# Ordering loaded operands of small products behind dense steps in a fused attention, RWKV and delta-rule block

## The chip, the core and the metric

The kernel runs on one core of one Trainium2 chip. The metric is the device time of one execution in microseconds, as the median of three runs. TensorE (PE in the rows) does the matrix products, VectorE (DVE), ScalarE (ACT) and GpSimd (POOL) the elementwise work, and SyncE (SP) issues most of the DMAs.

## What is computed

One block of a hybrid model: 1024 tokens, width 1024. The input is normed and projected by one large matrix (8176 columns); its columns feed three mixers (sparse attention "NSA" with 8 heads, an RWKV-7 recurrence with 8 heads, and a gated delta rule "GDN" with 4 heads) and three gates. The gated sum of the mixers is projected, added to the input, and a feed-forward layer of width 4096 follows. All in float32.

```python
proj = rms(x) @ w_in                       # nsa | rwkv | gdn | gates
# NSA: three branches per query; one over compressed keys and values
blk = t[:, :, cmp_idx, :] + cmp_pos[j]     # 63 windows of 32 tokens
hid = silu(blk.reshape(B, G, n_cmp, 32 * Dh) @ cmp_w1[j])
kc, vc = rms(hid @ cmp_w2[0]), hid @ cmp_w2[1]
ks, kw = rms(k_s), rms(k_w)                # selected and window branch
# GDN, per chunk
decay = exp(where(lower, gam[:, None] - gam[None, :], -inf))
a_mat = eye(C) + where(strict, (kb @ k.T) * decay, 0)
u, w = solve(a_mat, v * beta), solve(a_mat, kb * exp(gam))
qk = (q @ k.T) * decay
# RWKV: a state per head, a rank-one correction per token
# then
merged = g0 * (o_a @ wb0) + g1 * (o_b @ wb1) + g2 * (o_c @ wb2)
x = x + merged @ w_out
x = x + relu(rms(x) @ w_ff1)**2 @ w_ff2
```

## The kernel before

**Two kinds of work share TensorE.** *Dense steps* are the projections with 512-column products, each split in three products of high and low parts (`fps` tiles, line 97). *Small products* belong to the mixers (`mps` tiles, lines 97 and 101): chains of small matrix products with DVE, ACT or POOL work between them. The mixers are written as Python generators ("tasks"), which `yield` a delay at each point where something else should run. `Block.run` takes the task that is due; where none is due it emits a dense step (three products) instead. The clock of this game, `te.time`, counts estimated TensorE time of what was emitted. So a delay of 3.0 after a load means that about 3 us of dense products are emitted before the next small product. The delays stand in the tables `LAT` (RWKV), `GLAT` (GDN) and `NLAT` (NSA).

**What is emitted is not yet the order.** When the kernel is built, a scheduler sets the order on each engine, by priorities and by its own estimate of durations. Dense steps carry a lower priority (`delta`), so a small product may pass dense steps that were emitted ahead of it. `Tensor.note` adds an edge the other way: the first dense product of a step comes behind the last small one emitted (`anchor`). On the chip each engine works strictly in its order, so a product that waits holds all behind it.

**The stages.** RWKV (about 60 to 645 us of the trace): eight units; in each, a triangular inverse is made of 16-blocks by DVE (`inv_blocks`), written to DRAM and read back as `U16` and `T16`; `mm8(L16, T16)` (rows `T,L`), then `mm8(U16, X)` (rows `L,U`) and more steps widen it to 64-blocks, and four recurrence steps (`VS,AG`, `xs,U`, `VS,KB`, `VS,G`) use it. GDN (to about 1068 us): the same pattern with `gT`, `gX`, `gU` and 128-blocks, `mm4(X, T)` being the first product behind the load (rows `gT,gX`); the recurrence is `gZ,KQ`, `gxh,gU`, `gyb,gKg`. There a POOL step makes `gDs`, the decays without their diagonal, from `gD`. NSA preparation (about 1069 to 1160 us): four `_nsa_kv` tasks load keys and values (`kr`, `vr`, 256 KB each) and norm them (first product `ksq`, then `krb`, `vr`); `_nsa_compress` loads `posr` (16 KB), transposes it, and for keys and values in turn loads `kT` (1 MB), `cw1` (four loads of 512 KB) and `cw2` (64 KB), with 16 products `cw,xl`. Then 32 attention units follow. Dense work of the projection ends during them; the output stage and the feed-forward layer come last.

**Queues.** All loads named here go out on SP, `posr` and `kg` on POOL's queue, stores of finished dense tiles (`gates<-fst`) on ACT's.

## Time and profile before

| | us |
|---|---|
| median of three runs | 2536.28 |
| lowest, highest | 2533.8, 2540.54 |
| the profiled execution | 2527.64 |
| its span, first to last instruction | 2525.9 |
| PE busy in it | 2377.5 |
| mean granted TensorE clock | 0.965 |

The profiled execution took 1.7 us more than its span. A granted clock of 1.00 is 2.4 GHz, 0.5 is 1.2 GHz; a mean between them is a mixture over a stretch. Rows of waits name the engine that waited, what it wanted to do, and what it waited for. "x8" counts records: a float32 product of a small tile leaves two records.

### The profile page before, as it was taken

How to read it: one execution, taken by the hardware profiler on the slowest of the kernel's cores; microseconds unless marked ns; L12 is line 12 of the kernel's file. 1: busy time of each engine (PE TensorE's matmuls, PEld its weight loads, DVE VectorE, ACT ScalarE, POOL GpSimd, SP SyncE). 2: the span in 40 equal slices, each digit the busy share in tenths (PEclk: the TensorE clock that was granted, in tenths of full speed). 3: DMA queues.
4: the chain of work that ended last, by engine and by line, in shares of the span. 5: the costliest groups of instructions: out<-in, count | busy, mean ns of one | idle time of the engine just before them, and what ended most of it. 6: DMA issues, size and time to landing. Idle time of an engine off the chain costs nothing.

```text
span 2525.9 us, 37184 instructions
## 1 busy us (share of the span) xinstructions
PE 2377.5 (94%) x13589; PEld 1907.6 (76%) x13589; DVE 1472.0 (58%) x3197; ACT 1043.1 (41%) x2083; POOL 986.8 (39%) x975
## 2 busy tenths in 40 slices
PE   6979899999988999989999999999999998999999
PEld 4757676777776777777887777778888876788887
DVE  4586877663477567232556777766454436545444
ACT  5333433332344433225657665654332334423232
POOL 4444444333322121224545675344333346233232
PEclk9889889999999999989999999999999999999999
DMA  4222222222223122272213331014232354223232
GB/s 137 68 56 65 58 63 58 71 54 74 72 66 83 43 57 73 83 173 80 64 52 114 111 106 57 21 62 128 92 109 84 117 164 157 75 88 111 83 111 92
DMA packets 319718, 216.79 MB, mean 86 GB/s; under 512 B 78486, under 2 KB 273184, under 8 KB 319536
## 3 DMA queue, kind: packets, MB, share of 16 engines
q1 hardware_dynamic: 308672, 195.63, 27.3%
q10 hardware_dynamic: 9792, 17.83, 2.0%
q8 instruction: 107, 1.75, 0.3%
q0 software_dynamic: 1072, 0.96, 0.2%
q14 instruction: 75, 0.61, 0.1%
HBM read 178.16 MB, written 36.22 MB: 85 GB/s over the span
## 4 chain that ended last, share of the span: by engine, by line
PE 72%; DVE 13%; DMA 6%; ACT 4%; issue 2%; POOL 2%; SPq 0%; ACTq 0%; POOLq 0%; DVEq 0%
PE fps L97 53%; PE mps L97 15%; PE mps L101 3%; DVE inv_p L336 2%; DVE inv_u L338 1%; DVE gacc L882 1%; DVE BK L550 1%; DMA cw<-in_nsa_cmp_w_dram 1%; POOL wlo L259 1%; DMA lb<-inv 1%; ACT P L1349 1%; ACT whi L254 1%; DMA wraw<-in_w_branch_dram 1%; DVE ast L1344 1%; DMA gin<-gates 1%
## 5 line engine op out<-in xcount | busy, mean ns | idle before, releaser
L259 POOL TENSOR_TENSOR wlo<-wraw,whi 128x512 fp32r<-128x512 f32 (+2 forms) x408 | 530.0, 1302 | 878.9 <-ACT whi L254 848.5
L254 ACT CAST whi<-wraw 128x512 fp32r<-128x512 f32 (+1 forms) x408 | 286.6, 705 | 632.1 <-PE fps L97 444.8
L97 PE MATMUL fps<-hTh,whi 128*128 128x512 f32 x1024 | 447.3, 439 | 6.5 <-ACT rraw L424 3.5
L97 PE MATMUL fps<-hTh,wlo 128*128 128x512 f32 x1024 | 415.8, 410 | 1.3 <-POOL wlo L259 1.3
L97 PE MATMUL fps<-hTl,whi 128*128 128x512 f32 x1024 | 416.5, 408 | 0.0
L259 DVE TENSOR_TENSOR wlo<-wraw,whi 128x256 fp32r<-128x256 f32 (+1 forms) x207 | 129.7, 629 | 232.5 <-ACT whi L254 227.0
L97 PEld LDWEIGHTS fps<-hTh,whi 128*128 128x128 f32 x1024 | 200.9, 197 | 48.5 <-ACT rraw L424 3.6
L97 PEld LDWEIGHTS fps<-hTh,wlo 128*128 128x128 f32 x1024 | 200.0, 196 | 47.7 <-POOL wlo L259 2.2
L97 PEld LDWEIGHTS fps<-hTl,whi 128*128 128x128 f32 x1024 | 201.8, 197 | 32.3
L97 PE MATMUL fps<-h2h,whi 128*128 128x512 f32 x512 | 200.0, 391 | 1.3 <-DVE h2l L291 1.3
L1363 POOL TENSOR_SCALAR P<-P,ast 128x64 f32<-128x64 f32 (+5 forms) x128 | 137.2, 1088 | 160.0 <-DVE ast L1356 97.1
L97 PE MATMUL fps<-h2l,whi 128*128 128x512 f32 x512 | 199.6, 390 | 0.0
L97 PE MATMUL fps<-h2h,wlo 128*128 128x512 f32 x512 | 199.4, 390 | 0.0
L97 PE MATMUL fps<-whi,fl 128*128 128x512 f32 x512 | 191.0, 389 | 0.0
L97 PE MATMUL fps<-whi,fh 128*128 128x512 f32 x512 | 189.9, 391 | 0.0
L97 PE MATMUL fps<-wlo,fh 128*128 128x512 f32 x512 | 189.0, 389 | 0.0
L1442 DVE TENSOR_TENSOR acc<-fps,acc 128x512 f32<-128x512 f32 x160 | 106.7, 686 | 101.4 <-PE fps L97 101.0
L1349 ACT ACTIVATE P<-mps,ast 128x128 f32<-128x128 f32 (+4 forms) x256 | 124.9, 494 | 75.3 <-DVE ast L1347 45.5
L1344 DVE TENSOR_REDUCE ast<-mps 128x1 f32<-128x128 f32 (+4 forms) x256 | 109.0, 441 | 56.3 <-PE mps L97 53.5
L1392 DVE TENSOR_TENSOR PL<-mps,PH 128x512 fp32r<-128x512 f32 (+2 forms) x168 | 103.3, 619 | 47.7 <-ACT PH L1391 47.0
L1391 ACT CAST PH<-mps 128x512 fp32r<-128x512 f32 (+2 forms) x168 | 88.1, 533 | 63.5 <-PE mps L101 58.1
L97 PEld LDWEIGHTS fps<-h2h,whi 128*128 128x128 f32 x512 | 96.2, 188 | 21.5 <-DVE h2l L291 1.8
(465 smaller groups left out, 4802.0 us busy)
## 6 DMA issues: line engine op xcount, KB each, us to landing
wraw<-in_w_in_dram SPq DMA_DIRECT2D x152, 256.0 KB, 2.9
wraw<-in_w_ff_dram SPq DMA_DIRECT2D x128, 256.0 KB, 2.8
wraw<-in_w_ff_dram SPq DMA_DIRECT2D x64, 512.0 KB, 3.4
gates<-fst ACTq DMA_DIRECT2D x48, 256.0 KB, 2.0
wraw<-in_w_branch_dram SPq DMA_DIRECT2D x48, 256.0 KB, 3.2
gin<-gates SPq DMA_DIRECT2D x48, 256.0 KB, 3.2
wraw<-in_w_out_dram SPq DMA_DIRECT2D x16, 512.0 KB, 3.5
nsa_in<-fst ACTq DMA_DIRECT2D x20, 256.0 KB, 2.1
```

What stands on the lines that cost most here:

```text
L97: return self.note(self.nc.tensor.matmul(out, lhsT=lhsT, rhs=rhs, **kw))
L101: return self.note(self.nc.tensor.transpose(out, x, ident))
L254: nc.scalar.copy(hi, raw)
L259: eng.tensor_tensor(out=lo[:, x], in0=raw[:, x], in1=hi[:, x].bitcast(F32), op=OP.subtract)
L336: nc.vector.tensor_tensor(out=v, in0=lt[:n, s, None, s + 1:].to_broadcast([n, w, w]), in1=u[:n, s + 1:, s + 1:].rearrange("p t c -> p c t" ...
L338: nc.vector.tensor_reduce(out=u[:n, s, s + 1:], in_=v, axis=AX, op=OP.add)
L1344: nc.vector.tensor_reduce(out=(mx if i == 0 else mx2)[:, b:b + 1], in_=ps[:, :n], axis=AX, op=OP.max, negate=True)
L1349: nc.scalar.activation(out=Pt[:, c:c + n], in_=tiles[i][:, :n], func=AF.Exp, bias=mx[:, b:b + 1], accum_out=(sm if i == 0 else sm2)[:, b:b ...
L1363: eng.tensor_scalar(out=Pt[:, c:c + n], in0=Pt[:, c:c + n], scalar1=r[:, b:b + 1], scalar2=None, op0=OP.mult)
L1391: nc.scalar.copy(PH[:n, x0:x1], ps[:n, x0:x1])
L1392: tt(out=PL[:n, x0:x1], in0=ps[:n, x0:x1], in1=PH[:n, x0:x1].bitcast(F32), op=OP.subtract)
L1442: tt(out=acc[:, st, c0:c0 + 512], in0=ps, in1=acc[:, st, c0:c0 + 512], op=OP.add)
```

## The change

It has five parts.

1. `Tensor` gets a flag `held` and remembers the last dense product (`filled`). A task sets `held` when the operand of its next small product was loaded by DMA; that product is then placed behind the last dense product emitted before it. It is set at five points: RWKV's `mm8(L16, T16)`, GDN's `mm4(X, T)`, the norm of `kr`, the first `cw,xl`, and the norm of a query `q`.
2. `NLAT[1]` (behind the loads of `kr`, `vr`) goes from 3 to 8, `NLAT[2]` (behind the loads of the compression) from 6 to 14.
3. The compression's task moves from fifth place (order 4) to second (order 0.5), ahead of three of the four `_nsa_kv` tasks.
4. `posr` is loaded with the constants at the kernel's start.
5. GDN's `gDs` goes; `gD`, which keeps its diagonal, takes its place. `triS` goes with it.

```diff
-NLAT = (1.5, 3.0, 6.0, 0.3, 1.0, 3.0, 6.0, 0.6, 2.0, 0.8)
+NLAT = (1.5, 8.0, 14.0, 0.3, 1.0, 3.0, 6.0, 0.6, 2.0, 0.8)
@@ class Tensor
-        self.last = self.anchor = None
-        self.dense = False
+        self.last = self.anchor = self.filled = None
+        self.dense = self.held = False
@@ def note(self, ins)
         if not self.dense:
             self.fresh = ins.ins
-        elif self.anchor is not None:
+            if self.held and self.filled is not None:
+                self.tc.add_manual_dep(ins.ins, self.filled.name, self.EDGE, reason="behind the dense steps emitted before it")
+            self.held = False
+            return ins
+        self.filled = ins.ins
+        if self.anchor is not None:
             self.tc.add_manual_dep(ins.ins, self.anchor.name, self.EDGE, reason="dense step behind a small one")
             self.anchor = None
         return ins
@@ def constants(self)
+        self.posr = c.tile([64, 64], F32, name="posr")
+        nc.gpsimd.dma_start(out=self.posr, in_=a["nsa_cmp_pos"][0].rearrange("j l d -> (j l) d"))
         for n, k in (("nsa_q_norm", 1), ("nsa_k_norm", 3)):
@@ def _rwkv_unit
         yield LAT[12]
+        self.te.held = True
         ps = mm8(L16, T16, "i")
@@ def _gdn_unit
-        Ds = self.tl("gDs", 2)
-        nc.gpsimd.tensor_tensor(out=r4(Ds), in0=r4(Dm), in1=self.triS[:, None, :].to_broadcast([P, 4, P]), op=OP.mult)
         yield GLAT[2]
...
-                stt(out=LT[:, x], in0=pv[:, e, 0], scalar=nbn2[:, 2 * j + e:2 * j + e + 1], in1=Ds[:, x], op0=OP.mult, op1=OP.mult)
+                stt(out=LT[:, x], in0=pv[:, e, 0], scalar=nbn2[:, 2 * j + e:2 * j + e + 1], in1=Dm[:, x], op0=OP.mult, op1=OP.mult)
...
         yield GLAT[5]
+        self.te.held = True
         nc.scalar.copy(X, mm4(X, T))
@@ def nsa(self)
-            prep.append(self.task(self._nsa_compress(K2c, V2c), 4))
+            prep.append(self.task(self._nsa_compress(K2c, V2c), 0.5))
@@ def _nsa_kv
         yield NLAT[1]
+        self.te.held = True
         k = yield from self.norm64(kr, self.col["nsa_k_norm"][:, 1 + br:2 + br], "k", PSUM)
@@ def _nsa_compress
-        pr = self.tl("posr", 1, [64, 64])
-        nc.gpsimd.dma_start(out=pr, in_=a["nsa_cmp_pos"][0].rearrange("j l d -> (j l) d"))
+        pr = self.posr
...
             yield NLAT[2]
+            self.te.held = True
             hp = self.mps("o", 1)
@@ def query (in _nsa_attn)
             yield NLAT[5]
+            self.te.held = True
```

**What it moves.** The places below are from the built order. The changed file is eleven lines longer, so its dense products are at L98 and its transposes at L102, where the profile has L97 and L101.

SP at the start of NSA preparation, before (`kr` and `vr` are keys and values of one `_nsa_kv`, `kT` and `cw` the compression's operands):

```order
L1187 DMA kr<-nsa_in 128x512
L1189 DMA vr<-nsa_in 128x512
L1187 DMA kr<-nsa_in 128x512
L1189 DMA vr<-nsa_in 128x512
L1187 DMA kr<-nsa_in 128x512
L1189 DMA vr<-nsa_in 128x512
L1187 DMA kr<-nsa_in 128x512
L1189 DMA vr<-nsa_in 128x512
L1218 DMA kT<-nsa_in 64x2x1024
L1219 DMA kT<-nsa_in 64x2x1008
L1223 DMA cw_9975<-in_nsa_cmp_w_dram 64x8x256
```

The same place on SP with the change:

```order
L1196 DMA kr<-nsa_in 128x512
L1198 DMA vr<-nsa_in 128x512
L1227 DMA kT<-nsa_in 64x2x1024
L1228 DMA kT<-nsa_in 64x2x1008
L1232 DMA cw_9944<-in_nsa_cmp_w_dram 64x8x256
L1233 DMA cw_9944<-in_nsa_cmp_w_dram 64x8x256
L1232 DMA cw_9944<-in_nsa_cmp_w_dram 64x8x256
L1233 DMA cw_9944<-in_nsa_cmp_w_dram 64x8x256
L1235 DMA cw_9949<-in_nsa_cmp_w_dram 128x2x64
L1196 DMA kr<-nsa_in 128x512
L1198 DMA vr<-nsa_in 128x512
L1196 DMA kr<-nsa_in 128x512
```

The second `kr` moved from behind one `vr` to behind the seven loads of the compression's first half.

PE at the same stage, before (the first products behind the 2448th dense one; `ksq` is the square of the first `kr`):

```order
L97 MATMUL fps<-hTh,whi 128x512
L97 MATMUL fps<-hTl,whi 128x512
L97 MATMUL fps<-hTh,wlo 128x512
L101 MATMUL mps<-ident,posr 64x64
L97 MATMUL mps<-blk_9937,ksq 128x2 x4
L97 MATMUL fps<-hTh,whi 128x512 x2
L97 MATMUL fps<-hTl,whi 128x512
```

PE with the change, 39 dense products further on (the first `ksq` here is that of the first `kr`, the second that of the second):

```order
L98 MATMUL fps<-hTh,wlo 128x512
L98 MATMUL mps<-blk_9920,ksq 128x2 x4
L98 MATMUL fps<-hTh,whi 128x512
L98 MATMUL fps<-hTl,whi 128x512
L98 MATMUL fps<-hTh,wlo 128x512
L98 MATMUL mps<-blk_9920,ksq 128x2 x4
L98 MATMUL mps<-ident,krb 128x128 x4
```

The first `ksq` moved from the 2448th dense product to the 2487th, the second from the 2466th to the 2490th; the first three `cw,xl` moved from the 2466th to the 2502nd, and the transpose of `posr` stayed at the 2448th.

PE in RWKV behind the 561st dense product, where one unit's recurrence ends and the next unit's products begin, before:

```order
L97 MATMUL fps<-hTh,wlo 128x512
L97 MATMUL mps<-VS,G 64x64
L97 MATMUL mps<-VS,KB 64x64 x4
L97 MATMUL mps<-VS,G 64x64 x3
L97 MATMUL mps<-sums,rk 128x2
L97 MATMUL mps<-sums,sq 128x2
L97 MATMUL mps<-sums,rk 128x2
L97 MATMUL mps<-sums,sq 128x2
L97 MATMUL mps<-sums,rk 128x2
L97 MATMUL mps<-sums,sq 128x2
L97 MATMUL mps<-sums,rk 128x2
L97 MATMUL mps<-AG,BK 128x128 x4
```

The same place with the change:

```order
L98 MATMUL fps<-hTh,wlo 128x512
L98 MATMUL mps<-T_2524,L_2525 64x64
L98 MATMUL mps<-VS,G 64x64
L98 MATMUL mps<-VS,KB 64x64 x4
L98 MATMUL mps<-VS,G 64x64 x3
L98 MATMUL mps<-T_2524,L_2525 64x64 x15
L98 MATMUL mps<-sums,rk 128x2
L98 MATMUL mps<-sums,sq 128x2
```

The sixteen `T,L`, which stood last before the next dense product, moved ahead of `sums`, and `AG,BK` moved behind the next six dense products.

## Rows read from the trace of the kernel before

**Rows 1.** The page, part 1: busy time, share, instructions of each engine.

```profile
PE 2377.5 (94%) x13589; PEld 1907.6 (76%) x13589; DVE 1472.0 (58%) x3197; ACT 1043.1 (41%) x2083; POOL 986.8 (39%) x975
```

**Rows 2.** Waits of PE on DMAs: us in total, times, longest us.

```profile
PE mps L97 <- DMA cw<-in_nsa_cmp_w_dram: 7.3, 2, 6.0
PE mps L101 <- DMA posr<-in_nsa_cmp_pos_dram: 5.2, 1, 5.2
PE mps L97 <- DMA gT<-inv: 4.7, 3, 1.8
PE mps L97 <- DMA T<-inv: 0.8, 1, 0.8
```

**Rows 3.** Windows, PE: stretch, its us, busy (records), granted clock, DMA share, GB/s.

```profile
276.00:293.00 17.00, 13.00 (x95) 0.60 0.27 56
404.00:419.00 15.00, 10.98 (x86) 0.66 0.27 61
763.00:801.00 38.00, 30.28 (x172) 1.00 0.27 68
953.00:981.00 28.00, 23.55 (x113) 0.84 0.25 67
1069.00:1126.00 57.00, 44.23 (x219) 0.88 0.81 182
1339.00:1370.00 31.00, 28.56 (x173) 0.94 0.41 134
1740.00:1760.00 20.00, 20.00 (x90) 1.00 0.78 261
```

**Rows 4.** Timeline of PE, NSA preparation: start, us, instruction, idle before and releaser.

```profile
1075.19 0.31 PE L101 MATMUL mps<-ident,posr 64*64 64x64 f32 x1 [5.19 <-DMA posr<-in_nsa_cmp_pos_dram]
...
1091.26 2.90 PE L97 MATMUL mps<-cw,xl 128*126 128x256 f32 x6 [5.96 <-DMA cw<-in_nsa_cmp_w_dram]
```

**Rows 5.** Timeline of SP in the same stage: the last issue of `cw`.

```profile
1080.87 1.75 SPq L1224 DMA_DIRECT2D cw<-in_nsa_cmp_w_dram  x1
```

**Rows 6.** Tile `cw`: its loads' time from issue to landing.

```profile
DMA to landing us min/median/max: 8.6/12.3/15.3
```

**Rows 7.** Windows, DMA of all queues: stretch, us, SP busy, clock, DMA share, GB/s.

```profile
1068.00:1073.00 5.00, 1.00 0.83 191
1073.00:1078.00 5.00, 0.63 1.03 389
1078.00:1083.00 5.00, 0.69 0.98 233
1083.00:1088.00 5.00, 0.99 1.09 210
```

**Rows 8.** Timeline of ACT: the square of the first `kr`.

```profile
1074.99 0.63 ACT L1166 ACTIVATE ksq<-kr 128x512 f32<-128x512 f32 x1 [4.03 <-DMA kr<-nsa_in]
```

**Rows 9.** Timeline of PE in RWKV: five products that waited, and `T,L`.

```profile
278.60 0.39 PE L97 MATMUL mps<-sums,rk 128*128 128x2 f32 x2 [1.75 <-POOL rk L544]
285.70 0.85 PE L97 MATMUL mps<-VS,AG 128*64 128x64 f32 x4 [2.25 <-DVE VS L682]
...
287.48 2.00 PE L97 MATMUL mps<-T,L 64*64 64x64 f32 x29
...
408.32 1.77 PE L97 MATMUL mps<-AG,BK 64*128 64x128 f32 x8 [4.02 <-DVE BK L550]
...
449.46 0.34 PE L97 MATMUL mps<-VS,G 128*64 128x64 f32 x2 [2.40 <-DVE VS L699]
...
566.62 0.33 PE L97 MATMUL mps<-VS,G 128*64 128x64 f32 x2 [0.46 <-DVE VS L699]
```

**Rows 10.** Timeline of PE in GDN: the first unit's inverse, standing alone.

```profile
733.15 0.44 PE L97 MATMUL mps<-gT,gLT 32*32 32x32 f32 x16 [0.68 <-ACT gU L1017]
...
737.95 0.68 PE L97 MATMUL mps<-gT,gLT 64*64 64x64 f32 x8 [0.81 <-DVE gU L1038]
```

**Rows 11.** Lines, POOL: the removed step, count, busy and mean, idle before.

```profile
L957 POOL TENSOR_TENSOR gDs<-gD,triS 128x512 f32<-128x512 f32 x8 | 12.1, 1515 | 14.6 <-ACT gD L955 14.6
```

More of the change, by code (lines that the diff above doesn't have):

```diff
@@ L782, in gdn_tri @@
         nc = self.nc
-        self.tri, self.triS, self.triN = (self.tl(n, 1, [P, P]) for n in ("tri", "triS", "triN"))
-        for t, one, fill, base in ((self.tri, 1.0, 0.0, 0), (self.triS, 1.0, 0.0, -1), (self.triN, 0.0, NEG, 0)):
+        self.tri, self.triN = (self.tl(n, 1, [P, P]) for n in ("tri", "triN"))
+        for t, one, fill, base in ((self.tri, 1.0, 0.0, 0), (self.triN, 0.0, NEG, 0)):
             nc.gpsimd.memset(t, one)
```

## Prediction

> **What bounds the kernel now.** I read the page first, then PE's waits, then windows by stage, then timelines where the waits lie. TensorE is busy for 2377.5 of 2525.9 us [rows 1]; 148 us are left, and a stretch at half clock costs on top of that. So the time is PE's work, which the change leaves alone, plus PE's idle time, plus what the lower clock adds. A change of order can win only the last two. The waits on loads that the hold aims at are few: 7.3 us for `cw`, 5.2 for `posr`, 4.7 for `gT` in three waits, 0.8 for `T` [rows 2], 18.0 us or 0.7% of the span. The orders before and after are the same up to the 384th dense product and from the 3801st on, apart from a few transposes at the start, so only what lies between them can move. About 0.3% (7.6 us) is what a measurement of this kernel can tell from no change.
>
> **Part 1, NSA preparation: -3.6 us.** Before, the stretch from 1069 to 1126 us holds 57 - 44.2 = 12.8 us of idle PE, at a granted clock of 0.88 [rows 3]. The first wait is `posr`, from 1070.0 (1075.19 - 5.19) on; the second is 5.96 us for `cw` [rows 4]. With the change `posr` has long landed. PE then runs 42 dense products (39 and 3) at 0.222 us each (20 us for 90 [rows 3]), 9.3 us, the transpose of `posr` (0.31 [rows 4]) and the first `ksq`, an estimate of 0.8. So it stands at the second `ksq` at about 1080.4. That product needs the second `kr`, which the new order issues behind `kT` (1.04 MB) and all of the first `cw` (2.1 MB).
>
> When does it land? From the late side: the last `cw` before was issued at 1080.87 [rows 5], and no `cw` took more than 15.3 us [rows 6], so it landed by 1096.2. Six loads of 0.26 MB no longer stand ahead of it; at the 389 GB/s that they ran at [rows 7] that is 4.0 us, so 1092.2. The first `cw2` and `kr` itself, 0.33 MB, add 0.8: 1093. From the early side: the first `kr` and `vr` are moved by 1073, as is 0.17 MB of `kT`. The rest of `kT` at 233 GB/s takes 3.7 us, `cw` at 210 GB/s 10.0 us [rows 7], and 0.8 as above: 1087.5, rounded up 1088. I take 1091, nearer to the late side, since that starts from a landing and not from rates. ACT's square adds 0.63 [rows 8]. PE would wait from 1080.4 to 1091.6, 11.2 us (8.2 to 13.2), and by then `kT` and `cw` are there too, so the 1.4 us of the second half's `cw` wait (7.3 - 5.96) goes as well. Idle time goes from 12.8 to 11.2: -1.6. Three gaps become one. The clock in this stretch was below full for 0.12 x 57 = 6.8 us in all, part of it while PE stood; I take 2 back. Together -3.6, with ends of -8 and +1.
>
> A rule of the Trainium skill bears on this and speaks against the change. The loads of SP came out in their order before: the rate falls from 389 to 233 to 210 GB/s [rows 7] as `kr` and `vr`, then `kT`, then `cw` pass. The Trainium skill, "DMA: Bandwidth & Descriptors", section "Queues, rings and completion order", says that each DMA engine consumes the descriptors of a ring in ring order; by that rule the second `kr` cannot overtake the compression, and the trace agrees. The same page (section "Bandwidth") puts the limit of loads from HBM at about 358 GB/s for a core; by that figure the 3.1 MB ahead would take 8.8 us instead of the 13.7 above, an estimate of 1083 for the landing and a wait of about 3 us, which would make the sum 8 us better; the rows show 210 to 233 GB/s for these very loads.
>
> **Part 2, the hold in RWKV: -7.1 us.** Two places are bad before. At 278.60 and 285.70 PE waits 1.75 and 2.25 us for POOL and DVE, and at 408.32 4.02 us for DVE [rows 9]; each time it had sixteen `T,L` products and six dense ones left that stood behind the wait. The windows around them run at clocks of 0.60 and 0.66 [rows 3]. With the change `T,L` and the six dense products stand ahead of the product that waits. Six dense are 1.3 us; 29 of the 32 records of `T,L` took 2.00 us at a low clock [rows 9], so all are 2.2 there, half at full clock, 1.6 in the middle; and at the second place the `sums` about 1 more (an estimate). That is 2.9 and 3.9 us of cover against 4.0 of waits at each place; I take all 8.0 us, since the products behind `T,L` can fill what is short. The 0.8 for `T` [rows 2] goes too, since `T,L` now comes later. At half clock PE worked for about 11 us in the first window and 10 in the second (17 and 15 us at 0.60 and 0.66, idle time included); at full clock half of that is saved, 10 us. I take 4 of it, because long runs of small products remain in both places.
>
> Against this, at four places (dense counts 393, 513, 744, 978) `VS,G` now follows `xs,U` with nothing between, where `T,L` or `wa,up` stood. Two such pairs in the old order waited 2.40 and 0.46 us for DVE [rows 9]; at the mean, 1.43, four cost 5.7. Sum: -8.0 - 0.8 - 4 + 5.7 = -7.1. Ends: -15 (nothing lost at the four places) and +8 (the rival below).
>
> **Part 3, the hold in GDN: -2 us.** `gT,gX` moves later by 27 to 63 dense products in six units; for the first unit it stays at the 1554th, and its wait stays. So two of the three waits for `gT` can go. In the old order the inverse of one unit was woven into the recurrence of the one before, and there PE stood 38 - 30.3 = 7.7 us in one window and 28 - 23.6 = 4.4 in another [rows 3], the two waits included. In the new order the inverse stands alone after the recurrence, as the first unit's always did; that one waited 0.68 + 0.81 = 1.5 us [rows 10]. Four units now pay 1.5 that did not, 6.0; two are squeezed into 33 dense products each, with one dependent pair without cover, 1.5 + 1.4, 5.8 together. Idle: -12.1 + 11.8. The second window's clock was 0.84; I take 1.7 back. Sum -2, ends -7 and +5.
>
> **Part 4, attention: +2.5 us.** Longer delays in the preparation emit more dense steps there: the first query norm comes at the 2715th dense product instead of the 2664th, and the projection's dense work (3072) ends at the eleventh attention unit (counted from 0) instead of the thirteenth. Units without it keep PE less busy: from 1339 to 1370, three such units, PE stood 2.4 us at a clock of 0.94 [rows 3], 2.4 + 1.9 = 4.3 us, 1.4 a unit. One and a half to two more such units make +2.5 (0 to +5). From the 3399th dense product on the two orders run together again.
>
> **Part 5, the rest: 0.** `gDs` took 12.1 us of POOL [rows 11], and no PE wait names it: an end of -1 if some chain in GDN starts earlier. The load of `posr` at the start is one more small transfer on POOL's queue ahead of four others; what they fill is transposed behind the first tokens' norm, so 0; without that cover it would be one more such transfer, an estimate of +0.5. The hold before the query norm has no wait to remove.
>
> **Rivals.** *All the waits on loads go:* the second `kr` lands by 1080, since nothing forces the one queue to be full when it is issued. Then part 1 gains 12.8 + 4 instead of 3.6, and the sum is -23: 2513. The rates of [rows 7] speak against it. *RWKV gains nothing:* DVE, which ended three of the waits of [rows 9], sets the pace itself, so that the cover only moves PE's idle time behind the next product; part 2 is then about +1 and the sum -2: 2534. That the hold does not do what it says, because the scheduler had most of these products in the right place anyway (as `gT,gX` of the first unit), ends at the same time. *Slower:* the four pairs `xs,U`, `VS,G` without cover each cost the 2.40 of the worse row, 9.6. The clock falls with them: in the two windows of RWKV 8.0 us of waits came with 0.40 x 17 + 0.34 x 15 = 11.9 us of clock below full [rows 3], 1.5 for each us waited; since part of that lay in the waits themselves I take half, 0.7, so 9.6 x 0.7 = 6.8. Nothing of the old clock loss returns. Part 2 is then -8.8 + 16.4 = +7.6. With parts 1, 3 and 4 at -1.6, 0 and +2.5 the sum is +8.5: 2545. It decides from about 2.2 us a pair, clock included, where part 2 turns to a loss. For it: RWKV is the stage with the most small products. Against it: the last such pair waited 0.46.
>
> **How the numbers follow.** -3.6 - 7.1 - 2 + 2.5 = -10.2 us. Against the profiled 2527.6 that is 2517.4; that execution was 8.6 us below the median of 2536.3, so for the median 2526.1. Chances: the forecast 0.46, all waits gone 0.14, RWKV gains nothing 0.27, slower 0.13. Faster by over 0.3% means below 2528.7: seven tenths of the forecast's share, all of the first rival and a little of the second, 0.47. Slower means above 2543.9: 0.14 with a little of the second rival. The rest, 0.39, is within 0.3%. The range reaches from just below the first rival, 2511, to the third, 2545; the forecast's own range is 2520 to 2533.
>
> **What would show it.** In the profile after: no wait for `posr`; one wait of 8 to 13 us at a `ksq` in the preparation, ended by `kr` through ACT (right for part 1, and its absence the first rival); no wait of over 1 us at `sums`, `VS,AG` or `AG,BK` at the two places in RWKV, and the clock there above 0.8 (part 2); waits at `VS,G` behind `xs,U` (their size decides between forecast and slower); `gT,gX` waiting once, 1.6 us; the last third, from the 3801st dense product on, unchanged in length. The prediction is wrong if RWKV's length, from the 384th to the 1149th dense product, does not fall, or if the dense products behind the second `ksq` wait for weights.

## The result and the profile after

The changed kernel takes 2564.35 us (median of four runs, 2560.3 to 2578.22) against 2536.06: the ratio is 1.014, with an interval of 1.0111 to 1.0168. It is 28 us slower by the medians and 28 to 43 us by the ratio's interval, where 10 us faster was forecast; it lies above the range of the forecast, which ended at 2545.

The page, part 1, of the changed kernel (it answers to [rows 1]):

```profile
span 2564.3 us, 37182 instructions
PE 2394.0 (93%) x13589; PEld 1917.6 (75%) x13589; DVE 1465.6 (57%) x3197; ACT 1044.9 (41%) x2083; POOL 974.0 (38%) x965
```

The work of PE is the same 13589 instructions; 16.5 of the 38.4 us by which the span grew are busy time, that is, the same products at a lower clock (0.957 on the mean against 0.965), and 21.9 are idle time. Where they lie is read by cutting both traces at dense products at which the two orders stand level: the 384th and the 1149th (RWKV between them), the 2448th (GDN), the 2664th (the preparation, about) and the 3399th (attention beside other dense work). Windows of the kernel before, in this order (stretch, its us, PE busy and records, granted clock, DMA share, GB/s):

```profile
191.24:592.70 401.46, 379.24 (x3163) 0.92 0.26 63
592.70:1069.61 476.91, 441.60 (x2685) 0.96 0.25 67
1069.61:1162.34 92.73, 79.96 (x383) 0.93 0.63 150
1162.34:1537.94 375.60, 363.57 (x2101) 0.98 0.28 87
```

The same windows of the changed kernel:

```profile
196.99:605.49 408.50, 377.29 (x3162) 0.93 0.25 62
605.49:1080.46 474.97, 441.84 (x2686) 0.97 0.25 67
1080.46:1172.66 92.20, 73.51 (x355) 0.93 0.61 148
1172.66:1576.89 404.23, 379.22 (x2130) 0.95 0.26 81
```

RWKV is 7.0 us longer, GDN 1.9 shorter, preparation and attention together 28.1 longer (they share their small products differently, 383 records against 355 in the first, so they are read as one). Ahead of the 384th dense product, where the orders are alike, the two traces differ by 5.8 us, and the 20 profiles of this case have 174 to 183 us from the first dense product to that one: so much is chance in one trace. From the 3399th on the two are alike to 0.6 us, as forecast.

PE's waits in the preparation of the changed kernel (timeline; start, us, instruction, idle before it and what ended it):

```profile
1104.83 1.87 PE L98 MATMUL mps<-blk,ksq 128*128 128x2 f32 x8 [13.13 <-ACT ksq L1175]
1111.69 1.13 PE L98 MATMUL mps<-ident,krb 128*128 128x128 f32 x8 [0.79 <-DVE V2s L1211]
1143.12 0.67 PE L98 MATMUL mps<-cw,hidT 128*63 128x64 f32 x8 [0.98 <-DVE hidT L1252]
1147.03 0.24 PE L102 MATMUL mps<-ident,kn 64*128 64x64 f32 x1 [1.66 <-DVE kn L1148]
```

The one long wait at a `ksq` that was forecast is there, from 1091.70 to 1104.83, in place of the waits for `posr` and `cw` of [rows 4]. PE's waits in RWKV, grouped (what waited, for what; us in total, times, longest), of the kernel before:

```profile
PE mps L97 <- DVE VS L699: 6.5, 5, 2.4
PE mps L97 <- DVE BK L550: 4.0, 1, 4.0
PE mps L97 <- DVE VS L705: 3.8, 3, 1.7
PE mps L97 <- DVE VS L682: 2.3, 1, 2.3
PE mps L97 <- POOL rk L544: 1.8, 1, 1.8
PE mps L97 <- DMA T<-inv: 0.8, 1, 0.8
```

and of the changed kernel (its lines stand some nine further on):

```profile
PE mps L98 <- DVE VS L708: 8.1, 9, 2.3
PE mps L98 <- ACT L L637: 4.7, 2, 3.3
PE mps L98 <- DVE VS L714: 4.5, 3, 1.6
PE mps L98 <- ACT VS L614: 3.2, 2, 2.5
PE mps L102 <- POOL Y L744: 3.0, 3, 2.2
PE mps L98 <- DVE xs L699: 1.9, 1, 1.9
PE mps L98 <- DVE BK L558: 1.8, 1, 1.8
PE mps L98 <- DVE VS L691: 0.5, 1, 0.5
```

The waits that were to go did go: `rk` and `T` wholly, `BK` from 4.0 to 1.8, `VS` of the first recurrence product from 2.3 to 0.5, 6.6 us in sum. But `L`, `VS` of ACT, `Y` and `xs`, which were not waited for, now cost 12.8. In attention the groups that PE waits for are the same before and after, only larger: first before, then after.

```profile
PE mps L97 <- ACT P L1349: 5.9, 8, 1.7
PE mps L97 <- DVE PL L1392: 3.2, 3, 2.1
PE mps L97 <- ACT PH L1391: 1.3, 2, 1.0
```

```profile
PE mps L98 <- ACT P L1360: 12.0, 8, 2.7
PE mps L98 <- DVE PL L1403: 7.7, 7, 4.1
PE mps L98 <- ACT PH L1402: 3.4, 3, 1.6
```

### The profile page after: what moved, and what is told of

It reads as the page before. It is cut to its first block, busy times and chain, and to the rows that moved or that the text cites. A ratio compares the mean times of both kernels' runs of the same rounds, so it can differ in the third digit from the quotient of the medians.

```text
span 2564.3 us, 37182 instructions
## 1 busy us (share of the span) xinstructions
PE 2394.0 (93%) x13589; PEld 1917.6 (75%) x13589; DVE 1465.6 (57%) x3197; ACT 1044.9 (41%) x2083; POOL 974.0 (38%) x965
## 4 chain that ended last, share of the span: by engine, by line
PE 56%; DVE 5%; ACT 3%; DMA 3%; issue 1%; POOL 0%; SPq 0%; ACTq 0%; POOLq 0%; DVEq 0%
PE fps L98 44%; PE mps L98 9%; PE mps L102 3%; DMA wraw<-in_w_branch_dram 1%; ACT P L1360 1%; DVE ast L1355 1%; DVE inv_p L344 1%; DMA wraw<-in_w_in_dram 0%; ACT whi L262 0%; DVE gacc L891 0%; DMA vr<-nsa_in 0%; DVE PL L1403 0%; DVE inv_u L346 0%; DMA gates<-fst 0%; DVE P L1374 0%
## 5 line engine op out<-in xcount | busy, mean ns | idle before, releaser
L98 PE MATMUL fps<-hTh,whi 128*128 128x512 f32 x1024 | 451.5, 443 | 8.9 <-ACT whi L262 3.9
L98 PE MATMUL fps<-hTh,wlo 128*128 128x512 f32 x1024 | 416.2, 409 | 1.1 <-POOL wlo L267 1.1
L98 PE MATMUL fps<-hTl,whi 128*128 128x512 f32 x1024 | 416.5, 409 | 0.0
L98 PEld LDWEIGHTS fps<-hTh,whi 128*128 128x128 f32 x1024 | 200.9, 197 | 52.1 <-ACT whi L262 5.0
L98 PEld LDWEIGHTS fps<-hTh,wlo 128*128 128x128 f32 x1024 | 201.0, 196 | 48.5 <-POOL wlo L267 2.0
L98 PEld LDWEIGHTS fps<-hTl,whi 128*128 128x128 f32 x1024 | 202.3, 198 | 31.4
L98 PE MATMUL fps<-h2h,whi 128*128 128x512 f32 x512 | 200.0, 391 | 0.0
L98 PE MATMUL fps<-h2l,whi 128*128 128x512 f32 x512 | 199.5, 390 | 0.0
L98 PE MATMUL fps<-h2h,wlo 128*128 128x512 f32 x512 | 199.5, 390 | 0.0
L98 PE MATMUL fps<-whi,fl 128*128 128x512 f32 x512 | 191.3, 390 | 0.0
L98 PE MATMUL fps<-whi,fh 128*128 128x512 f32 x512 | 189.4, 390 | 0.0
L98 PE MATMUL fps<-wlo,fh 128*128 128x512 f32 x512 | 189.1, 390 | 0.0
L98 PEld LDWEIGHTS fps<-h2h,whi 128*128 128x128 f32 x512 | 96.2, 188 | 20.0 <-DVE h2l L299 0.2
```

The source lines that it names most:

```text
L98: return self.note(self.nc.tensor.matmul(out, lhsT=lhsT, rhs=rhs, **kw))
```

## The experiments

Ratios are to runs of the kernel before on the same chip beside them, with a 95% interval; 0.1% is 2.5 us. They, and not the quotients of medians from different chips, are what is compared. The diffs show the lines that an edit is about, with "..." for what is left out; where a hold is set, `Tensor` has the flag as in the change. Single traces carry several us of chance (above), so a stage is judged by several runs that share its order. Three theories stood at the start. **D:** the longer delays use up dense products in the preparation, and attention then runs dry (a *dry piece* is the run of small products between the last dense product of the projection and the first of the output stage: 132 before, 211 after). **P:** the new order of loads makes keys and values late. **H:** the holds themselves cost.

**The delays, alone and taken back.** First the kernel before with the two longer delays alone:

```diff
-NLAT = (1.5, 3.0, 6.0, 0.3, 1.0, 3.0, 6.0, 0.6, 2.0, 0.8)
+NLAT = (1.5, 8.0, 14.0, 0.3, 1.0, 3.0, 6.0, 0.6, 2.0, 0.8)
```

> The kernel before with nothing but the two longer delays (NLAT[1] 8, NLAT[2] 14). In the built order the small products that stand in one piece between the last dense product of the projection (the 3072nd) and the first of the output stage are 251; the kernel before has 132, the changed kernel 211. Theory D (the dry stretch is what the change costs): from the 3072nd to the 3399th dense product the changed kernel lost 11.6 us more to idle PE and 14.1 us more to the lower clock than the kernel before, 25.7 us for 79 more dry products, 0.33 us each; 119 more cost 39 us, less up to 10 us that longer delays can save at the loads of the preparation: 2565 to 2577. Theory P (the cost is that keys and values wait behind the compression's loads, and the holds; the delays alone cost nothing): 2530 to 2540.

Measured: 2538.89 us, ratio 1.0026 (1.001 to 1.0041), 3 to 10 us slower. Then the changed kernel with the old delays:

```diff
-NLAT = (1.5, 8.0, 14.0, 0.3, 1.0, 3.0, 6.0, 0.6, 2.0, 0.8)
+NLAT = (1.5, 3.0, 6.0, 0.3, 1.0, 3.0, 6.0, 0.6, 2.0, 0.8)
```

> The changed kernel with the two delays of before (3 and 6); all else of the change stays. The dry piece has 95 products instead of 211. Theory D: 116 fewer at 0.33 us give back up to 38 us, of which the preparation, with fewer dense products ahead of the second key norm, loses 4 to 6 again: 2530 to 2540. Theory P: 2558 to 2570, since loads and holds are as in the changed kernel.

Measured: 2562.11 us, ratio 1.0128 (1.0105 to 1.015). Theory D falls twice as the main cause: with 251 dry products the loss is 7 us and not 30, and with 95 the changed kernel is as slow as with 211 within the intervals. The 25.7 us that the trace shows behind the 3072nd dense product are real, but most of them were put down to the wrong cause.

**Each hold alone.** RWKV's:

```diff
 yield LAT[12]
+self.te.held = True
 ps = mm8(L16, T16, "i")
```

> The kernel before with nothing but the hold at RWKV's first widening product. Outside RWKV the order on PE is that of before. Theory R (the hold takes away 6.5 us of waits and puts 15.9 us of new ones at L,U, wa,up, Y and xs,U in their place, as the two traces show): 5 to 10 us slower, 2541 to 2546. Theory N (the two traces differ there by chance; the hold is worth nothing): 2534 to 2538. The prediction: 7 us faster, 2529.

Measured: 2536.76 us, ratio 1.0027 (1.0011 to 1.0043), 3 to 11 us slower: theory R by the ratio (the time itself lies in theory N's range, but the runs of before beside it had 2532), and a miss of the prediction. With the early load of `posr` added, since that alters 212 lines of PE's order in RWKV:

```diff
 yield LAT[12]
+self.te.held = True
...
+self.posr = c.tile([64, 64], F32, name="posr")
+nc.gpsimd.dma_start(out=self.posr, in_=a["nsa_cmp_pos"][0].rearrange("j l d -> (j l) d"))
```

> The kernel before with RWKV's hold and the early load of posr. In RWKV this gives PE the order of the changed kernel (with the hold alone 212 of its lines stand elsewhere). Theory S (the early load disturbs the scheduler's choice and with it the order in RWKV; the two traces with this order were 7 and 16 us longer there): 8 to 15 us slower than before. Theory H (the hold sets the price and posr adds nothing): as with the hold alone, 3 to 6 us slower; less if the wait of 5.2 us for posr is gained.

Measured: 2534.99 us, ratio 1.0021 (1.0 to 1.0042). By time this is H; by its trace RWKV took 416.6 us, which is S. So the opposite was run too, the changed kernel with `posr` loaded in the preparation again:

```diff
-pr = self.posr
+pr = self.tl("posr", 1, [64, 64])
+nc.gpsimd.dma_start(out=pr, in_=a["nsa_cmp_pos"][0].rearrange("j l d -> (j l) d"))
```

> The changed kernel with posr loaded in the preparation again. PE's order in RWKV becomes that of the run with RWKV's hold alone. Theory S (hold and early posr together give an order in RWKV that costs some 14 us, of which the hold alone is 4): RWKV from the 384th to the 1149th dense product back from 408 to 419 us to 400 to 406, the time 8 to 12 us less than the changed kernel: 2552 to 2556 against 2531 to 2536 of before; up to 5 us of that lost if posr's own wait returns. Theory H (the two traces differ by chance): 2560 to 2566.

Measured: 2566.37 us, ratio 1.0144 (1.0118 to 1.017): theory S falls. In this trace RWKV takes 414.7 us with the very order that took 404.8 in the run with RWKV's hold alone. Taken together, the seven profiles of kernels with RWKV's hold have 404.8 to 418.9 us there (mean 413.2, PE idle 29.7), the thirteen without it 397.1 to 407.7 (mean 401.3, idle 25.0), the early `posr` on both sides. By the profiles the hold costs 12 us, 5 of them idle time and 7 longer busy time of the same products. The times of the two runs with this hold alone say less, 5 to 7 us (0 to 11), so its size is known only as 5 to 12.

The query's hold:

```diff
 yield NLAT[5]
+self.te.held = True
 QH = self.tl("QH", 2, [P, 2, 512], F32R)
```

> The kernel before with nothing but the hold at the norm of a query. PE's order is that of before up to the 2664th dense product; from then on five of the eight query norms stand 7 to 15 dense products later. Theory Q (a later query norm starts the next four attention units later, and these wait on ACT and DVE): both traces with this hold lost 7 to 9 us more than before between the 3130th and the 3399th dense product, so 5 to 9 us slower than before. Theory Z (the query has slack): 0 to 2 us.

Measured: 2538.69 us, ratio 1.0041 (1.0021 to 1.006), 5 to 15 us slower: theory Q, but not yet its reason. PE's waits in attention with this hold alone (1172 to 1563 us of its trace):

```profile
PE mps L98 <- ACT P L1356: 6.9, 9, 1.7
PE mps L98 <- DVE PL L1399: 6.2, 5, 4.5
PE mps L98 <- ACT PH L1398: 5.8, 5, 3.7
```

`PL` and `PH`, the operands of the product of probabilities and values, go from 4.5 to 12.0 us, and the stretch from the 2664th to the 3399th dense product from 375.6 to 390.4. All of the loss lies behind the 3072nd dense product, the last of the projection: from there to the 3399th PE takes 207.3 us against 191.3, ahead of it 183.1 against 184.3. There the sixth query norm, which before stood ahead of the output stage's first dense product, stands behind fifteen of them (3087th), and the seventh moves from the 3264th to the 3273rd. In the changed kernel these two stand at the 3088th and 3273rd with the hold, at the 3072nd and 3264th without it (run below), and there too the difference lies behind the 3072nd alone (229.5 against 214.4 us).

To tell lateness from the hold itself, the hold was kept and the delay ahead of it cut:

```diff
-NLAT = (1.5, 3.0, 6.0, 0.3, 1.0, 3.0, 6.0, 0.6, 2.0, 0.8)
+NLAT = (1.5, 3.0, 6.0, 0.3, 1.0, 0.1, 6.0, 0.6, 2.0, 0.8)
```

> The kernel before with the hold at the query norm, and the delay behind the query's load cut from 3.0 to 0.1, which brings six of the eight query norms back to or ahead of their old place (2652 to 3444 against 2664 to 3444). Theory L (what costs 8 to 10 us is that the next four units get their query later): 0 to 3 us slower than before. Theory E (the hold itself costs, wherever the norm stands, because it reshuffles the products of the units behind it, and these then wait on ACT and DVE): 6 to 12 us slower.

Measured: 2545.53 us, ratio 1.0066 (1.0045 to 1.0087), even slower than theory E's 6 to 12, with 389.2 us in the same stretch. Earlier query norms elsewhere do not help. But the run does not decide between the theories: in its trace the sixth norm, behind which the loss begins, still stands at the 3084th dense product, and 203.2 us pass from the 3072nd to the 3399th. Whether the lateness of this one norm costs, or the new order of the units behind it, is not shown.

The two holds of the preparation, loads in the old order:

```diff
 yield NLAT[1]
+self.te.held = True
...
 yield NLAT[2]
+self.te.held = True
```

> The kernel before, loads in its order, with nothing but the holds at the first key norm and the first compression product. The first cw,xl moves from the 2466th to the 2499th dense product. If cover is what the wait for cw lacks (6.0 us before): 33 dense products at 0.222 us are 7.3 us of cover, 4 to 8 us faster, clock included. If the wait is only handed on to the steps behind it (hid, kn, the first query): 0 to 2 us either way.

Measured: 2530.48 us, ratio 0.9997 (0.9979 to 1.0014): no change, the wait is handed on.

**The order of loads alone.**

```diff
-prep.append(self.task(self._nsa_compress(K2c, V2c), 4))
+prep.append(self.task(self._nsa_compress(K2c, V2c), 0.5))
```

> The kernel before with nothing but the compression's task in second place. Theory O (the second keys wait behind 3.1 MB of loads, one long wait at the second ksq, longer than the three it replaces): the version with the old delays waited 14.3 us there and was 7.7 us longer in the preparation: 5 to 10 us slower. The prediction's step for the loads (11.2 us of idle in place of 12.8): -2 to +2.

Measured: 2534.54 us, ratio 1.0024 (1.0006 to 1.0042), 2 to 11 us slower: theory O by the ratio, not the prediction's step. Theory P has this much in it and no more.

**GDN.** Both edits:

```diff
-Ds = self.tl("gDs", 2)
...
-                stt(out=LT[:, x], in0=pv[:, e, 0], scalar=nbn2[:, 2 * j + e:2 * j + e + 1], in1=Ds[:, x], op0=OP.mult, op1=OP.mult)
+                stt(out=LT[:, x], in0=pv[:, e, 0], scalar=nbn2[:, 2 * j + e:2 * j + e + 1], in1=Dm[:, x], op0=OP.mult, op1=OP.mult)
...
         yield GLAT[5]
+        self.te.held = True
```

> The kernel before with nothing but GDN's two edits (the hold at gT,gX, and no gDs). Outside GDN the order on PE is that of before up to the start of the preparation. The prediction: 2 us faster, 2534. The two traces: GDN from the 1149th to the 2448th dense product took 2.0 us less. If all waits for gT went and nothing came in their place: 5 us faster, 2531.

Measured: 2522.38 us, ratio 0.9967 (0.9953 to 0.9982), 5 to 12 us faster, more than each of the three expected. The removed POOL step alone:

```diff
-Ds = self.tl("gDs", 2)
-nc.gpsimd.tensor_tensor(out=r4(Ds), in0=r4(Dm), in1=self.triS[:, None, :].to_broadcast([P, 4, P]), op=OP.mult)
...
```

> The kernel before without gDs, nothing else. PE's order is that of before throughout. The prediction: 0 (12.1 us of POOL's time that PE never waits for). If it is this edit that gains the 10 us of the run with both GDN edits: 2521 to 2525.

Measured: 2524.19 us, ratio 0.998 (0.9964 to 0.9996). The hold alone, `gDs` kept:

```diff
 yield GLAT[5]
+self.te.held = True
 nc.scalar.copy(X, mm4(X, T))
```

> The kernel before with the hold at gT,gX, gDs kept. The prediction's step: -2. If the hold is what gains in the run with both GDN edits: 8 to 10 us faster than before, 2521 to 2525. In the traces GDN's own stretch is no shorter with the hold (474 to 475 us with and without), which speaks for 0.

Measured: 2532.6 us, ratio 1.0017 (1.0 to 1.0034). The removed POOL step gains 5 us (1 to 9), and the hold gains nothing. The stage says the same: from the 1149th to the 2448th dense product nine profiles with neither edit average 474.4 us (471.7 to 476.9), three without `gDs` and without the hold 469.4 (469.0 to 469.8), seven with both edits 474.5, and the one with the hold alone 481.1. In this stage the removed step leaves PE's order in the traces as it was, so the gain does not come from the order.

How a step that PE never waits for can cost is seen on DVE. The inverse of a unit is a chain of short steps `inv_p` there. Before, one of them ran beside a `gDs` of POOL (timelines of DVE and POOL, kernel before) and ended 0.35 us behind it:

```profile
714.89 1.29 DVE L336 TENSOR_TENSOR inv_p<-lb,inv_u 32x196 f32<-32x196 f32 x1
714.55 1.28 POOL L957 TENSOR_TENSOR gDs<-gD,triS 128x512 f32<-128x512 f32 x1 [2.19 <-ACT gD L955]
```

The same step of the same unit without `gDs` (timeline of DVE):

```profile
715.60 0.49 DVE L342 TENSOR_TENSOR inv_p<-lb,inv_u 32x196 f32<-32x196 f32 x1
```

On the whole DVE is busy for 275.0 us in the stage before and 271.3 without `gDs`. That this makes up the 5 us was not tested. The waits of PE in this stage with the hold alone show what replaces the DMA waits of [rows 2]:

```profile
PE mps L102 <- DVE gT L1022: 6.7, 2, 4.2
PE mps L98 <- ACT gU L1024: 4.7, 7, 0.7
```

`gT` is no longer waited for from DRAM but one step further down its chain, 11.4 us in sum where 5.4 stood (4.7 for the load, 0.7 for `gU`). That the time with both edits (0.9967) is better than these two suggest is not explained; its GDN stage is not shorter.

**Halves and sums.** The changed kernel without the holds of RWKV and GDN, and with `gDs` back:

```diff
 yield LAT[12]
-self.te.held = True
...
+Ds = self.tl("gDs", 2)
...
 yield GLAT[5]
-self.te.held = True
```

> All of the change from NSA preparation on (loads of the compression early, both delays, early posr, holds at ksq, cw and the query), nothing in RWKV and GDN. The parts alone so far, each against its own runs of before: query hold +8 to +10, delays +7, order of loads +4 to +6, the two other holds -0.2. Theory A (they add): 2531 + 20 to 22 = 2551 to 2553. Theory I (they make each other worse, in the dry piece that the delays lengthen and the query hold delays): 2560 to 2570, which is then most of the changed kernel's loss.

Measured: 2566.2 us, ratio 1.0136 (1.0109 to 1.0163). The other half, loads, delays and holds of NSA as before:

```diff
-NLAT = (1.5, 8.0, 14.0, 0.3, 1.0, 3.0, 6.0, 0.6, 2.0, 0.8)
+NLAT = (1.5, 3.0, 6.0, 0.3, 1.0, 3.0, 6.0, 0.6, 2.0, 0.8)
...
-            prep.append(self.task(self._nsa_compress(K2c, V2c), 0.5))
+            prep.append(self.task(self._nsa_compress(K2c, V2c), 4))
...
 yield NLAT[1]
-self.te.held = True
...
 yield NLAT[2]
-self.te.held = True
...
 yield NLAT[5]
-self.te.held = True
```

> The other half: RWKV's hold, GDN's two edits and the early posr; loads, delays and holds of NSA as before. By the parts alone: +4 (RWKV's hold with posr) and -10 (GDN): 2523 to 2528. If the interaction that the sum of the parts lacks (the changed kernel is 28 us slower, the parts alone sum to 17 to 20) lies in RWKV and GDN: 2536 to 2545.

Measured: 2537.64 us, ratio 1.0022 (1.0007 to 1.0036), in the second of the two ranges: beside RWKV's hold the gain of GDN's edits is not seen. And the changed kernel without the query's hold:

```diff
 yield NLAT[5]
-self.te.held = True
 QH = self.tl("QH", 2, [P, 2, 512], F32R)
```

> The changed kernel without the hold at the norm of a query. Theory A (parts add): 8 to 10 us less than the changed kernel's 2564: 2554 to 2557. Theory I (the query hold costs more beside the longer delays, since the next four units then start late where no dense product is left to fill in): 15 to 25 less, 2539 to 2549.

Measured: 2550.62 us, ratio 1.0078 (1.0055 to 1.01). Within their intervals the two halves add up to the whole, 1.36 and 0.22% against 1.4%; but the NSA half alone is as slow as the whole, so beside it the edits of RWKV and GDN together cost nothing that the time can tell. Inside the NSA half the parts alone sum to 0.9% (0.41, 0.26, 0.24, -0.03) of 1.36, so they make each other worse, as theory I said of the sum; but without the query's hold the changed kernel gets back 14 us by the medians and 16 by the ratios, at the lower edge of theory I's range.

Theory D was given a last chance on the other side: GDN's edits with a lower share of dense steps in the first sixteen units, so that the dry piece has 61 products.

```diff
+self.share = 0.6
 self.run(lambda: mark[15] >= 2)
+self.share = 1.0
 self.end_mixed()
```

> The kernel before with GDN's two edits, and in the first sixteen attention units a share of 0.6 instead of 1.0, that is, fewer dense steps repaid for each us of small products. Dense steps then last longer: the dry piece has 61 small products instead of 132. Theory D, by the run with the two longer delays (119 more dry products, 7 us): 71 fewer give 4 us back, so 13 to 14 us faster than before, 2517. If dense steps are as well spent early as late: as with GDN's edits alone, 9 to 10 us faster, 2521.

Measured: 2524.33 us, ratio 0.9987 (0.9973 to 1.0001): nothing gained over GDN's edits alone, and by the ratio less than either theory expected.

**All holds out.** The changed kernel with delays, loads, `posr` and `gDs` as changed, without the five holds:

```diff
 yield LAT[12]
-self.te.held = True
...
 yield GLAT[5]
-self.te.held = True
...
 yield NLAT[1]
-self.te.held = True
...
 yield NLAT[2]
-self.te.held = True
...
 yield NLAT[5]
-self.te.held = True
```

> The changed kernel without any of the five holds; longer delays, early loads of the compression, early posr and no gDs stay. The dry piece has 219 products (changed kernel 211, before 132). Theory E (the holds carry the loss: RWKV's 7 to 12 us, GDN's 3, the query's 8 to 14): 18 to 29 us less than the changed kernel's 2564: 2535 to 2546. Theory P (delays and load order carry it): 2552 to 2564.

Measured: 2532.54 us, ratio 0.9996 (0.9975 to 1.0017), faster than theory E's range. The whole loss goes with the holds. Its windows (RWKV, GDN, preparation, attention):

```profile
190.16:597.91 407.75, 380.96 (x3163) 0.92 0.25 62
597.91:1067.67 469.76, 437.19 (x2685) 0.98 0.25 68
1067.67:1169.13 101.46, 85.18 (x399) 0.88 0.57 137
1169.13:1546.74 377.61, 363.33 (x2085) 0.97 0.28 86
```

Preparation and attention still take 479.1 us against 468.3 of before, the price of delays and load order; GDN takes 469.8 us, as in the other profiles without `gDs` and hold. With the dry piece at 219 products attention takes 377.6 us, which leaves to D no more than that price.

**A version that beats both.** The kernel before, without `gDs` and with the early load of `posr`:

```diff
-Ds = self.tl("gDs", 2)
...
+self.posr = c.tile([64, 64], F32, name="posr")
+nc.gpsimd.dma_start(out=self.posr, in_=a["nsa_cmp_pos"][0].rearrange("j l d -> (j l) d"))
```

> The kernel before without gDs and with the early load of posr, nothing else. gDs alone gave 5 us. If the early posr gains what two runs showed in the preparation (2 to 3 us less idle than before's 12.8): 6 to 8 us faster than before, 2523 to 2526. If posr's wait is only handed on to the wait for cw: as without gDs alone, 4 to 5 us faster.

Measured: 2516.8 us, ratio 0.995 (0.9923 to 0.9976), 6 to 19 us faster than the kernel before. The windows of GDN and of the preparation, and PE's waits in the latter:

```profile
587.96:1056.96 469.00, 435.39 (x2686) 0.98 0.25 68
1056.96:1147.05 90.09, 79.88 (x383) 0.94 0.66 155
```

```profile
PE mps L98 <- DMA cw<-in_nsa_cmp_w_dram: 8.1, 2, 7.3
PE mps L98 <- ACT ksq L1173: 2.0, 1, 2.0
```

The wait for `posr` is gone and only 2.5 us of it come back at `cw` and `ksq`: 10.2 us of idle PE against 12.8. With the 5 us of `gDs` that explains 8 us; the medians differ by 15 and the ratio by 13, more than both expectations, and the rest is not explained.

## Why the prediction was wrong

The sign that the prediction named for being wrong came: RWKV, from the 384th to the 1149th dense product, grew by 7.0 us.

**The step that failed** is a term put at nothing. Part 2, and part 5 in its sentence on the query norm, asked which waits a hold removes; part 2 costed the new place of a held product only where it left two others side by side, and part 5 gave it no cost. They did not ask what the old place was worth. In the runs the five holds carry the whole loss (ratio 1.014 with them, 0.9996 without). In the built order the first `T,L` of the eight RWKV units stands at the dense products 342, 393, 561, 645, 792, 890, 1008 and 1128; with the hold at 342, 456, 561, 684, 792, 915, 1023 and 1133. Its first user, `xs,U`, hardly moves (476 to 498 and 714 to 720 in two units, not at all in six). So what lies between them, the chain's slack, 83, 69, 64, 48 and 48 dense products in the five units that move, falls to 42, 36, 39, 33 and 43. Passing the dense steps was no accident to be mended: it ran a long chain early, and the load had nearly always landed (0.8 us of waits on `T` in all [rows 2]). For that wait the hold trades the slack.

What the lost slack costs is seen behind the second unit's `T,L`. Before, it runs from 197 us on, and its follower `L,U` meets no wait (timeline of PE, kernel before):

```profile
198.11 0.68 PE L97 MATMUL mps<-T,L 64*64 64x64 f32 x17
201.28 0.79 PE L97 MATMUL mps<-L,U 64*64 64x64 f32 x18
```

With RWKV's hold alone it runs at 225 us, then `sums`, six dense products, `AG,BK` and `VS,AG`, and then PE stands (timeline of PE):

```profile
224.73 1.15 PE L98 MATMUL mps<-T,L 64*64 64x64 f32 x32
229.60 0.45 PE L98 MATMUL mps<-VS,AG 128*64 128x64 f32 x6
233.36 1.98 PE L98 MATMUL mps<-L,U 64*64 64x64 f32 x32 [3.31 <-ACT L L635]
```

`L` is ACT's copy of the product of `T,L`. On ACT it now stands behind the end of the former unit (timeline of ACT in the same run, where `yg` and `Y` belong to that unit's output):

```profile
229.02 0.63 ACT L735 ACTIVATE yg<-Y 128x512 f32<-128x512 f32 x1 [2.31 <-DVE Y L733]
230.66 1.28 ACT L737 ACT_TABLE_LOAD   x1
232.16 0.56 ACT L747 COPY yg<-mps 128x512 f32<-128x512 f32 x1
232.72 0.58 ACT L635 COPY L<-mps 128x512 f32<-128x512 f32 x1
```

ACT first waits 2.31 us for `Y`, then loads a table, and so on; the copy starts 6.8 us after `T,L` ended. PE had 4.2 us of other work (225.88 to 230.05), but cover on PE does not count the queue of the engine that must act in between. That this is the cause of the other new waits (`VS` of ACT, `Y`, `xs`) is argued from their kind and was not shown one by one.

**Part 1, preparation (-3.6):** the mechanism was right. One wait at the second `ksq` was forecast from 1080.4 on for 11.2 us, within 8.2 to 13.2; with the stage 10.9 us later in this trace that is 1091.3, and it came at 1091.7 for 13.13. During it all queues together moved 265 GB/s:

```profile
1091.70:1104.80 13.10, 0.00 (x0) 0.66 1.09 265
```

The second `ksq` waited behind the compression's loads, as the consumption of a ring in its order by the Trainium skill lets expect ("DMA: Bandwidth & Descriptors", section "Queues, rings and completion order"); the trace agrees, since that `kr` of 0.26 MB left SP at 1092.64 us, behind all seven, and the wait for it lasted to 1104.83. By the figure of about 358 GB/s on the same page of the Trainium skill (section "Bandwidth") the wait was estimated at about 3 us; the rows differ from it both ways, 389 GB/s in [rows 7] and 265 here, and the 13.13 us decide. The term was mis-sized in what came after: three more waits of 0.8 to 1.7 us, shown above, and two of 1.0 and 1.1 at dense products, so that idle time is 18.7 us and not 11.2, and by itself the load order costs 2 to 11 us where 1.6 of idle and 2 of clock were to be won. The forecast's own condition, no `cw` waits behind the long one, held.

**Part 2, RWKV (-7.1):** the named waits went (6.6 of 8.8), and the four pairs `xs,U`, `VS,G` cost 1.6 more (6.5 to 8.1) where 5.7 was set. The sum failed by the 12.8 us of waits that had no row, and by the clock: 4 us were to come back, but the clock's cost (half of PE's busy time in stretches at half clock) is 34.5 us on the mean of the seven held profiles against 25.3.

**Part 3, GDN (-2):** right in sum by chance. The hold was given a gain of 2 and costs 4 to 7 (474.4 to 481.1 with `gDs`, 469.4 to 474.5 without, 4 in time); it moves `gT,gX` in seven units, not in six. The removed `gDs` was given nothing because no PE wait names it, and it gains 5. Part of the way is the DVE steps shown above; in PE's waits only those for `gT` by DMA (4.7 us in three to 2.5 in two) and for `KQ` (2.6 to 0.5) fall clearly, while one for DVE's `gT` (1.9) is new.

**Part 4, attention (+2.5):** in attention itself the delays were near (without holds it is 2.0 us longer, within 0 to +5), but with the preparation they cost more than was set: 8.5 us in the trace of the delays alone (468.3 to 476.8), 3 to 10 in time. The failed step here is the sentence of part 5 that the hold before the query norm has no wait to remove, taken as no cost: it costs 14 us of preparation and attention in the traces (468.3 to 482.6 alone, 482.6 to 496.4 in the changed kernel) and 10 to 16 in time. Where the loss lies is shown; why the moved norms cost so much stays open.

**Part 5:** the early `posr` was set to 0 at the start, and nothing speaks against it (up to the 384th dense product 174 to 182 us with it, 175 to 183 without). **The rivals:** the third, slower, named one right stage and the wrong pairs; it gave 2545, since it knew nothing of the query. The second called DVE the end of three waits of [rows 9]; it ended four of the five. That the hold does not do what it says is refuted by the orders. The sum as the profiles give it: RWKV +12, query +14, the two holds of the preparation about +4 (482.6 us for preparation and attention without the query's hold, 479.1 without any), delays and load order +11, GDN 0: 41, where the ratio's interval gives 28 to 43; with RWKV's hold as the times have it, 5 to 7, it is 34 to 36. No run tells the parts of this sum better than to some 5 us each.

## What to carry to other kernels

A scheduler that lets a small product pass filler work gives it slack; before an edge takes that away, count how far ahead of its first user it stood and how often it really waited. A removed wait of under 1 us is no reason to move a chain up to 41 products closer to its user, as the hold did in RWKV. And cover on the waiting engine is not enough: the engine that works between two products has a queue of its own, and what stands in that queue at the new place must be looked up too. Last, a step that TensorE never waits for can still hold up an engine that it does wait for, as `gDs` held up `inv_p`.

## What was not expected of the hardware

The lower clock cost more than the waits that came with it. In RWKV the held profiles have 4.7 us more idle time on the mean and 9.2 us more cost of the lower clock (34.5 against 25.3, worked out as half of PE's busy time in stretches at half clock); PE's busy time itself grew by 7.2 us. That is 1.5 to 2 us for each us waited, where 0.5 to 0.7 had been assumed. It is a comparison of two groups and not a rule: among the thirteen profiles without the hold the one with the least idle time (22.2 us) lost 29.1 us to the clock, and the one that lost least (19.6) had 25.4 us of idle time. And the clock varies between executions with the same order: the first stretch up to the 384th dense product took 174 to 183 us, with 13 to 26 us of it lost to the clock. So an order is judged by several profiles, not by one.

VectorE and GpSimd got in each other's way. The `inv_p` step shown above took 1.29 us beside a `gDs` of 1.28 us and 0.49 us where none ran.
